# A recurrent mixer's triangular solve in packed halves on ScalarE, GpSimd and TensorE, and a second weight buffer for early queries

## The chip, the cores and the metric

One NeuronCore of a Trainium2 chip runs the whole program. The engines are TensorE (PE; its weight loads are listed as PEld), VectorE (DVE), ScalarE (ACT), GpSimd (POOL) and SyncE (SP), each with a queue that it works off in order, and 16 DMA engines. The metric is the device time of one launch in microseconds (us). [...]

## What is computed

One layer of a decoder for 1024 prompt tokens and 64 sample tokens, as tiles 0 to 7 of 128 tokens and tile 8 of 64:

```
proj = rmsnorm(h) @ w_in                      # retention part and RWKV part
o_ret = retention(q, k, v)                    # chunks of 128 tokens, state between chunks
for t: sa = S @ (-kk[t])                      # RWKV-7, 8 heads of 64
       S = S * exp(log_w[t]) + outer(sa, kk[t]*a[t]) + outer(v[t], k[t]);  y[t] = S @ r[t]
h = h + concat(o_ret, o_rw) @ w_out
q = rmsnorm(h) @ peer_wq; s = q . keys        # 8 heads x 2 x 128 keys
e, gsm = top 16 of the sums of the two top 16 lists          # 128 experts for each token
h = h + sum_e gelu(x . u_tab[e]) * gsm_e * v_tab[e]
h = h + sigmoid(rmsnorm(h) @ ple_gate) * (p @ ple_proj);  y = rmsnorm(h)
```

The RWKV recurrence of a 128-token chunk is a triangular system for each head: with the strictly triangular matrix Q of the chunk, U solves (1 - Q) U = X, and the state and y follow from U.

## The kernel before

**Stages.** The program is written as generators that are stepped in turn, and a scheduler then sets each engine's order from the dependencies, the order of writing and its own model of durations. From 0 to about 545 us the projections of tiles run (`group_a`), with the mixer of tile 0. Then `group_b` runs the mixers of tiles 1, 8, 2, 3, 4, 5, 6, 7: at each step one yield of the solve and end of one tile (`cur`), one of the beginning of the next tile (`nxt`), one of the output projection of a finished tile (`c_rows`), and one of `early`. About 1868 us the queries of tiles 2 to 7 begin (`c_query`). Then the first 96 of 128 blocks of the dense experts are computed (`hidden`: 24 matmuls each), beside the top-k of tiles 2 to 7 and the gates of tiles 4 to 7 (`gates`: one-hot rows `oh` by VectorE, scaled by ScalarE, multiplied by TensorE into `pwt`). About 2819 us `dense_fused` and then `dense_stored` begin; the end (`ple`) starts about 3771 us.

**The gathers.** Tiles 0, 1, 8 (in `early`) and 2, 3 (later) take their experts by indirect DMA: GpSimd issues `grow` (512 KB, 128 rows) at L1126, VectorE multiplies it with x and sums (L1140, table u) or adds it to an accumulator (L1154, table v). For 0, 1, 2, 3 that is 128 of each table, for tile 8 it is 64 of each: 1152 gathers. The early ones have four `grow` buffers (five for tile 8, whose query is done). In the queues of GpSimd and VectorE they stand among the instructions of `group_b`.

**The early queries** (`early_query`) make the scores of tiles 0, 1 and 8. For each of 16 key sets a weight `ewq` of 512 KB is loaded, 8 matmuls `epq` are made with it, then one with the keys. Those of tiles 1 and 8 run in `group_b`, with one buffer `Wq` for the weights: the next load waits for the last matmul on the one before.

**The solve.** In `rw_mix` after `yield "chain"`, Z (128 x 8 heads x 128) starts as 1 plus Q's diagonal blocks of 2 (L824 on VectorE, L825 on GpSimd). Five levels m = 2, 4, 8, 16, 32 double the block, each in two groups of four heads (s = 0, 1): TensorE transposes Z (`trz`, L837), ScalarE copies it to `Tt` (L839), TensorE multiplies N (the transpose of Q) with the second half of each block (`pG`, L842), VectorE masks the product into `G` (L844), TensorE multiplies (`pZG`, L849), and VectorE adds the result into Z (L851). After five levels Z holds the inverses of two blocks of 64; U is then made in two halves (L901, L895, L897 on VectorE, L901, L903). Tiles 0 to 7 have five levels, tile 8 two.

Of the kernel before, what the change touches and what calls it, by code (L numbers as in the profile page):

```python
# [44 lines left out]
def consts():  # L45
# [27 lines left out]
    for i, m in enumerate(LEVELS):  # L73
        for qq in range(64):
            b = qq // m
            lev[b * 2 * m:b * 2 * m + m, i, qq] = 1.0
# [134 lines left out]
class K:  # L211
# [46 lines left out]
    def setup_mix(self, es):  # L258
# [18 lines left out]
        self.Sb = [[cp.tile([128, 4, 128], F32, name=f"S{a}{b}") for b in range(2)] for a in range(3)]  # L277
        for a in self.Sb:
            for b in a:
                nc.gpsimd.memset(b, 0.0)  # L280
        self.Sret = self.Swkv = None
# [364 lines left out]
    def group_b(self, tiles, early):  # L646
# [3 lines left out]
        with ExitStack() as e:  # L650
# [6 lines left out]
                                  ("PC", [64, 8, 8], F32, 1), ("Z", h8, F32, 2), ("N", h8, F32, 2), ("Tt0", [128, 4, 128], F32, 1),  # L657
                                  ("Tt1", [128, 4, 128], F32, 1), ("G0", [128, 4, 64], F32, 1), ("G1", [128, 4, 64], F32, 1)])
# [35 lines left out]
    def rw_mix(self, t):  # L694
# [123 lines left out]
        N = wp.tile([128, 8, n], F32, name="N", bufs=b2)  # L818
        self.transposes_n(N, Q[:, :, 0], n)
        yield  # L820
        Z = wp.tile([128, 8, n], F32, name="Z", bufs=b2)
        bd = self.c("bdiag2", n)[:, None, :n].to_broadcast([n, 8, n])
        idb = self.c("ident", n)[:, None, :n].to_broadcast([n, 8, n])
        nc.vector.tensor_tensor(Z[:n, :, :n], Q[:n, :, 0, :n], bd, op=OP.mult)  # L824
        nc.gpsimd.tensor_tensor(Z[:n, :, :n], Z[:n, :, :n], idb, op=OP.add)  # L825
        yield "chain"
        lev = self.c("lev").rearrange("p (l q) -> p l q", l=5)
        nq = n // 2
        for li, m in enumerate(LEVELS):
            if smp and m >= 8:  # L830
                break
            Zs = Z[:n, :, :n].rearrange("p h (c s m) -> p h c s m", s=2, m=m)[:, :, :, 1, :]
            Tt, G, pz = [None] * 2, [None] * 2, [None] * 2
            for s in range(2):
                p = self.ps("trz", hb[s]).rearrange("p (a b) -> p a b", a=4)
                for j in range(4):
                    nc.tensor.transpose(p[:n, j, :n], Z[:n, 4 * s + j, :n], self.c("ident", n)[:, :n])  # L837
                Tt[s] = wp.tile([128, 4, n], F32, name=f"Tt{s}")
                nc.scalar.activation(Tt[s][:n, :, :n], p[:n, :, :n], AF.Copy)  # L839
                p = self.ps("pG", hb[s])[:, :256].rearrange("p (h q) -> p h q", h=4)  # L840
                for j in range(4):
                    nc.tensor.matmul(p[:n, j, :nq], N[:n, 4 * s + j, :n], Zs[:, 4 * s + j], start=True, stop=True)  # L842
                G[s] = wp.tile([128, 4, n // 2], F32, name=f"G{s}")
                nc.vector.tensor_tensor(G[s][:n, :, :nq], p[:n, :, :nq], lev[:n, li, None, :nq].to_broadcast([n, 4, nq]), op=OP.mult)  # L844
                yield
            for s in range(2):
                p = self.ps("pZG", hb[s])[:, :256].rearrange("p (h q) -> p h q", h=4)
                for j in range(4):
                    nc.tensor.matmul(p[:n, j, :nq], Tt[s][:n, j, :n], G[s][:n, j, :nq], start=True, stop=True)  # L849
                pz = p[:n, :, :nq].rearrange("p h (c m) -> p h c m", m=m)  # L850
                nc.vector.tensor_tensor(Zs[:, 4 * s:4 * s + 4], Zs[:, 4 * s:4 * s + 4], pz, op=OP.add)  # L851
                yield
# [357 lines left out]
    def early(self, wp):  # L1210
# [4 lines left out]
        for t in E0[1:]:  # L1215
# [327 lines left out]
```

## Time and profile before

| | us |
|---|---|
| median of 3 runs | 3937.49 (3921.43 to 3937.65) |
| the profiled execution | 3941.76 |
| its span | 3940.0 |
| PE busy | 3367.7 (85%) |
| DVE busy | 2961.7 (75%) |
| POOL busy | 2339.6 (59%) |
| ACT busy | 1225.5 (31%) |

The span is the time from the first to the last instruction of the profiled execution. A busy time is the sum of an engine's instructions; "PEclk" is the TensorE clock that was granted, as a share of full speed, and the DMA share is the mean busy share of the 16 DMA engines. A wait is put down to what released it last. A stage is read from its own busy shares and waits, and the share of an engine over the whole span says little about one stage.

### The profile page before, as it was taken

The page shows a single profiled execution, that of the slowest core. Times are in us where ns is not written, and L with a number is a line of the kernel's source. Part 1 is how long each engine was busy: PE and PEld are TensorE (multiplying, and loading weights), DVE is VectorE, ACT ScalarE, POOL GpSimd, SP SyncE. Part 2 cuts the span into 40 slices and gives each one's busy share as a digit, 9 for nine tenths or more (in the row PEclk, how much of TensorE's full clock was granted, in tenths as well). Part 3 has the DMA queues.
Part 4 walks back from the last instruction along what each step waited for, and adds up shares of the span by engine and source line. Part 5 has one row for each costly group of instructions (what it writes and reads, how often), then busy time and mean ns, then how long its engine had stood idle before and what let it go on. Part 6 is the DMA issues. An engine that isn't in the chain of part 4 may idle for free.

```text
span 3940.0 us, 52682 instructions
## 1 busy us (share of the span) xinstructions
PE 3367.7 (85%) x17749; PEld 2768.7 (70%) x17749; DVE 2961.7 (75%) x5764; ACT 1225.5 (31%) x2247; POOL 2339.6 (59%) x2051
## 2 busy tenths in 40 slices
PE   8798985777869776885899899999699988999978
PEld 7687984645747664763788678888588866677757
DVE  4454488977697689886659999987777777777774
ACT  4232221011111111111232266777422333333322
POOL 5353175544454536554567757886488777777740
PEclk9799995666977567676999999999899999999989
DMA  7267568898868878789998748899899999999962
GB/s 256 72 194 234 168 209 266 277 302 267 295 229 285 299 269 283 265 278 332 331 350 295 245 171 302 306 347 344 324 343 341 334 362 357 358 362 349 339 230 70
DMA packets 473864, 1107.20 MB, mean 281 GB/s; under 512 B 74555, under 2 KB 191545, under 8 KB 467642
## 3 DMA queue, kind: packets, MB, share of 16 engines
q0 software_dynamic: 165888, 604.05, 43.0%
q1 hardware_dynamic: 245694, 393.26, 30.5%
q10 hardware_dynamic: 62012, 106.52, 7.2%
q8 instruction: 141, 2.31, 0.2%
q14 instruction: 129, 1.06, 0.1%
HBM read 997.17 MB, written 106.43 MB: 280 GB/s over the span
## 4 chain that ended last, share of the span: by engine, by line
PE 45%; DVE 22%; DMA 16%; issue 7%; POOL 6%; ACT 2%; SPq 0%; ACTq 0%; POOLq 0%; DVEq 0%
PE py L1294 14%; DVE grow L1140 4%; DVE gacc L1154 3%; PE ph L325 3%; PE ph L326 3%; PE ph L327 3%; POOL grow L1126 3%; DMA ewq<-in_wq 2%; PE epq L1194 2%; DMA grow<-in_pv,eid 2%; DMA grow<-in_pu,eid 2%; POOL vl L300 2%; DMA ft<-fd 1%; DVE oh L1240 1%; PE ewo L610 1%
## 5 line engine op out<-in xcount | busy, mean ns | idle before, releaser
L1126 POOL DMA_INDIRECT grow<-in_pv,eid x576 | 569.8, 989 | 507.3 <-DVE gacc L1154 309.4
L1126 POOL DMA_INDIRECT grow<-in_pu,eid x576 | 568.7, 987 | 435.2 <-DVE grow L1140 287.9
L1154 DVE SCALAR_TENSOR_TENSOR gacc<-grow,ac,gacc 128x1024 f32<-128x1024 f32 x571 | 731.8, 1282 | 89.5 <-DMA grow<-in_pv,eid 84.3
L1140 DVE SCALAR_TENSOR_TENSOR grow<-grow,gacc 128x1024 f32<-128x1024 f32 x576 | 691.1, 1213 | 125.0 <-DMA grow<-in_pu,eid 118.3
L1294 PE MATMUL py<-ah,vh 128*128 128x512 f32 x1024 | 408.1, 399 | 40.3 <-ACT ah L296 27.1
L1294 PE MATMUL py<-ah,vl 128*128 128x512 f32 x1024 | 407.1, 403 | 34.1 <-POOL vl L300 34.0
L325 PE MATMUL ph<-cx,uh 128*128 128x512 f32 x1024 | 406.4, 397 | 7.2 <-ACT geh L1262 7.2
L326 PE MATMUL ph<-cx,uh 128*128 128x512 f32 x1024 | 406.4, 397 | 0.0
L327 PE MATMUL ph<-cx,ul 128*128 128x512 f32 x1024 | 405.5, 396 | 1.0 <-POOL ul L300 1.0
L1294 PE MATMUL py<-al,vh 128*128 128x512 f32 x1024 | 405.3, 396 | 0.0
L300 POOL TENSOR_TENSOR vl<-vraw,vh 128x640 fp32r<-128x640 f32 (+2 forms) x224 | 325.4, 1457 | 53.1 <-ACT vh L296 49.3
L300 POOL TENSOR_TENSOR ul<-uraw,uh 128x1024 fp32r<-128x1024 f32 x128 | 308.6, 2412 | 64.5 <-ACT uh L296 62.3
L296 ACT ACTIVATE vh<-vraw 128x640 fp32r<-128x640 f32 (+2 forms) x224 | 154.9, 692 | 393.8 <-PE py L1294 238.3
L1294 PEld LDWEIGHTS py<-ah,vl 128*128 128x128 f32 x1024 | 194.1, 190 | 98.4 <-POOL vl L300 56.1
L1294 PEld LDWEIGHTS py<-ah,vh 128*128 128x128 f32 x1024 | 194.6, 190 | 96.5 <-ACT vh L296 28.7
L1298 DVE TENSOR_TENSOR yT<-yT,py 128x512 f32<-128x512 f32 x216 | 147.4, 684 | 151.5 <-PE py L1294 151.1
L325 PEld LDWEIGHTS ph<-cx,uh 128*128 128x128 f32 x1024 | 194.7, 190 | 48.4 <-ACT geh L1262 8.8
L1294 PEld LDWEIGHTS py<-al,vh 128*128 128x128 f32 x1024 | 194.0, 189 | 43.7
L327 PEld LDWEIGHTS ph<-cx,ul 128*128 128x128 f32 x1024 | 194.9, 190 | 41.6 <-POOL ul L300 1.9
L326 PEld LDWEIGHTS ph<-cx,uh 128*128 128x128 f32 x1024 | 195.0, 190 | 39.1
L296 ACT ACTIVATE uh<-uraw 128x1024 fp32r<-128x1024 f32 x128 | 135.2, 1056 | 246.1 <-PE ph L326 128.5
L300 POOL TENSOR_TENSOR wl<-wraw,wh 128x1024 fp32r<-128x1024 f32 x45 | 110.5, 2455 | 138.8 <-ACT wh L296 138.7
(400 smaller groups left out, 7833.3 us busy)
## 6 DMA issues: line engine op xcount, KB each, us to landing
uraw<-in_puT SPq DMA_DIRECT2D x128, 512.0 KB, 4.8
vraw<-in_pvd SPq DMA_DIRECT2D x152, 320.0 KB, 6.1
cw<-in_w_out SPq DMA_DIRECT2D x128, 256.0 KB, 5.1
wd<-wst ACTq DMA_DIRECT2D x32, 1024.0 KB, 13.1
wt<-wd SPq DMA_DIRECT2D x64, 512.0 KB, 8.0
wraw<-in_w_ret SPq DMA_DIRECT2D x48, 512.0 KB, 4.7
ewq<-in_wq SPq DMA_DIRECT2D x48, 512.0 KB, 6.7
gd<-geh ACTq DMA_DIRECT2D x96, 256.0 KB, 5.0
```

The lines of the kernel that those rows point to most:

```text
L296: nc.scalar.activation(hi, src, AF.Copy)
L300: nc.gpsimd.tensor_tensor(lo, src, hi.bitcast(F32), op=OP.subtract)
L325: mm(out, lh(k), rh(k), start=first and k == 0, stop=False)
L326: mm(out, lh(k), rl(k), start=False, stop=False)
L327: mm(out, ll(k), rh(k), start=False, stop=last and k == nk - 1)
L610: nc.tensor.matmul(p[:n], oT[k // 4][:, k % 4, :n], w, start=k == 0, stop=k == 7)
L1126: nc.gpsimd.indirect_dma_start(out=g, out_offset=None, in_=src, in_offset=bass.IndirectOffsetOnAxis(ap=self.eid[t][:, j:j + 1], axis=0))
L1140: nc.vector.scalar_tensor_tensor(g[:, c], g[:, c], 1.0, x[:, c], op0=OP.mult, op1=OP.mult, accum_out=hv[:, i, j:j + 1])
L1154: nc.vector.scalar_tensor_tensor(y[:, c], g[:, c], ac[:, j:j + 1], y[:, c], op0=OP.mult, op1=OP.add)
L1194: nc.tensor.matmul(p[:, :n], w[:, k], xT[:, k, :n], start=k == 0, stop=k == 7)
L1294: nc.tensor.matmul(p, lh[:, b, :], rh, start=b == 0 and j == 0, stop=b == nb - 1 and j == 2)
L1298: nc.vector.tensor_tensor(yT[:, d, :], yT[:, d, :], p, op=OP.add)
```

## The change

1. **The solve.** Z is kept in two packed halves (`Zt[0][:, 0]` the first halves of all blocks, `[:, 1]` the second ones) in one of two buffers Z0, Z1 that swap at each level. The mask moves from the product to N: GpSimd makes `Nm` (128 x 256) ahead (`mask`). ScalarE copies `pG` to `G` in two instructions of 64 partitions, into the diagonal quarters of a tile that was set to zero once. The transposes take two heads at once (two instead of four), TensorE adds the old half by a product with the identity (256 columns) in front of the two products of `Tt` and `G`, so that ScalarE only copies the sum out (`new`), and GpSimd copies the unchanged half to the other buffer (`old`), each in two instructions for m below 64. A sixth level m = 64 joins the two blocks of 64, with no mask and no copy by GpSimd. U then comes from one round (`pU`, 16 matmuls, one copy). VectorE has no part in the levels. The state product S0 is made ahead of the levels.
2. **Buffers.** `Wq` in the pool of the early queries has two buffers, and the queries of tiles 1 and 8 use both. `Tt`, `G`, Z, N and one of the states have fewer or smaller ones.

The rest is unchanged. The core of the diff (line numbers of the kernel after are 2 to 53 higher):

```diff
@@ rw_mix
-        lev = self.c("lev").rearrange("p (l q) -> p l q", l=5)
-        nq = n // 2
-        for li, m in enumerate(LEVELS):
...
-            for s in range(2):
-                p = self.ps("trz", hb[s]).rearrange("p (a b) -> p a b", a=4)
-                for j in range(4):
-                    nc.tensor.transpose(p[:n, j, :n], Z[:n, 4 * s + j, :n], self.c("ident", n)[:, :n])
...
-                nc.vector.tensor_tensor(G[s][:n, :, :nq], p[:n, :, :nq], lev[:n, li, None, :nq].to_broadcast([n, 4, nq]), op=OP.mult)
-                yield
...
-                nc.vector.tensor_tensor(Zs[:, 4 * s:4 * s + 4], Zs[:, 4 * s:4 * s + 4], pz, op=OP.add)
-                yield
+        def mask(i):
+            if i < len(steps) and levels[steps[i][0]] < 64:
...
+                Nm[i] = wp.tile([128, 4, nq], F32, name="Nm", bufs=1 + b2)
+                nc.gpsimd.tensor_tensor(Nm[i][:n].rearrange("p h (c m) -> p h c m", m=m),
...
+        old = lambda d, a: nc.gpsimd.tensor_copy(d, a)
+        new = lambda d, a: nc.scalar.activation(d, a, AF.Copy)
...
+        for i, (li, s) in enumerate(steps):
...
+            for j in range(4):
...
+                if m == 64:
+                    nc.tensor.matmul(po_, N[64:, h, 0:64], Zl[64:, 1, h], start=True, stop=True)
+                else:
+                    nc.tensor.matmul(po_, Nm[i][:n, j], Zl[:, 1, h], start=True, stop=True)
...
+                for e in (0, 64):
+                    es_ = slice(e, e + 64)
+                    nc.scalar.activation(G[es_, :, es_], p[es_, :256].rearrange("p (a b) -> p a b", a=2)[:, :, es_], AF.Copy)
+            if m < 64:
+                moved(old, Zl[:, 0, 4 * s:4 * s + 4], m, 0, s)
+            mask(i + 2)
...
+            for j in range(0, 4, w):
+                f = Zl[:, 0, 4 * s + j:4 * s + j + w].rearrange("p h q -> p (h q)")
+                nc.tensor.transpose(p[:nq * w, j // w, :n], f, idn)
+            nc.scalar.activation(Tt[s][:nq * w, :, :n], p[:nq * w, :4 // w, :n], AF.Copy)
+            yield
...
+            for s in range(2):
...
+                nc.tensor.matmul(p[:n, :, :nq], idn, zs, start=True, stop=False)
...
+                for j in range(0, 4, w):
+                    nc.tensor.matmul(p[:n, j:j + w, :nq], Tt[s][:nq * w, j // w, :n], G4[:nq * w, j:j + w, :nq], start=False, stop=j + w == 4)
+                if m < 64:
+                    moved(new, p[:n, :, :nq], m, 1, s)
+                else:
+                    new(zs, p[:n, :, :nq])
+                yield
@@ early, build
-            for _ in self.early_query(wp, t, "Wq", 1, ("Wq", "xT")):
+            for _ in self.early_query(wp, t, "Wq", 2, ("Wq", "xT")):
...
-            self.layout(ep0, [("V", [128, D], F32, 2), ("W", [128, D], F32, 1), ("xy", [128, D], F32, 1), ("Wq", [128, D], F32, 1), ("xT", [128, D], F32, 1)])
+            self.layout(ep0, [("V", [128, D], F32, 2), ("W", [128, D], F32, 1), ("xy", [128, D], F32, 1), ("Wq", [128, D], F32, 2), ("xT", [128, D], F32, 1)])
```

What stands in the queues at three places, before and after (a row is a line of the kernel, an operation, out<-in, its shape and how many follow one another):

VectorE, the first levels of tile 4's solve, before; `grow` rows are sums of the gather of tile 1:

```order
L1140 SCALAR_TENSOR_TENSOR grow,hv<-grow,gacc 128x1024 x13
L844 TENSOR_TENSOR G_10375<-pG,cstb 128x256
L844 TENSOR_TENSOR G_10409<-pG,cstb 128x256
L1140 SCALAR_TENSOR_TENSOR grow,hv<-grow,gacc 128x1024 x4
L851 TENSOR_TENSOR Z<-Z,pZG 128x128x2
L1140 SCALAR_TENSOR_TENSOR grow,hv<-grow,gacc 128x1024
L851 TENSOR_TENSOR Z<-Z,pZG 128x128x2
```

VectorE at the same place, after:

```order
L800 TENSOR_TENSOR Kq<-pab,cstb 128x512
L1207 SCALAR_TENSOR_TENSOR gacc<-grow,ac,gacc 128x1024 x3
L814 TENSOR_TENSOR nbk<-ptk,rn_10060 128x512
L1193 SCALAR_TENSOR_TENSOR grow,hv<-grow,gacc 128x1024 x16
L1034 TENSOR_TENSOR hnx<-hnx,pgt 128x512
```

The solve's rows are gone from the queue, and the gather beside this tile is 28 sums further back, still at the end of tile 0's list (`gacc`) before tile 1's begins.

GpSimd, tile 4 from the start of Z to the end of the levels, before:

```order
L974 TENSOR_TENSOR hnx<-hnx,bv 128x512
L825 TENSOR_TENSOR Z<-Z,csta 128x1024
L1126 DMA grow<-in_pu,eid_65 128x1024 x67
L290 TENSOR_SCALAR hnr<-hnss 128x8
L291 TENSOR_TENSOR hnr<-hnr,halves 128x8
```

GpSimd in the levels m = 2 to 8 of the same tile, after:

```order
L1179 DMA grow<-in_pu,eid_65 128x1024 x4
L869 COPY Z_10743<-Z_10626 128x32x4 x2
L1179 DMA grow<-in_pu,eid_65 128x1024 x2
L848 TENSOR_TENSOR Nm<-N,cstb 128x256
L869 COPY Z_10743<-Z_10626 128x32x4 x2
L848 TENSOR_TENSOR Nm<-N,cstb 128x256
L1179 DMA grow<-in_pu,eid_65 128x1024 x2
L869 COPY Z_10904<-Z_10743 128x16x8 x2
```

One run of 67 gathers becomes runs of one to eight with the solve's masks and copies between them.

TensorE in the third of the four tiles' gates, before (`ph` are matmuls of `hidden`):

```order
L327 MATMUL ph<-cx_13025,ul 128x512
L1245 MATMUL pwt<-oh_20393,oh_20394 128x128 x4
L1245 MATMUL pwt<-oh_20412,oh_20413 128x128 x4
L325 MATMUL ph<-cx_13025,uh 128x512
L326 MATMUL ph<-cx_13026,uh 128x512
```

TensorE at the same gates, after:

```order
L1298 MATMUL pwt<-oh_20733,oh_20734 128x128 x4
L1298 MATMUL pwt<-oh_20752,oh_20753 128x128 x4
L1298 MATMUL pwt<-oh_20771,oh_20772 128x128 x4
L1298 MATMUL pwt<-oh_20790,oh_20791 128x128 x4
L1298 MATMUL pwt<-oh_20809,oh_20810 128x128 x4
```

Of the 128 groups of gates, the last 80 now stand behind the last `ph` of the first 96 blocks; before, no more than the last 16 did.

## Rows read from the trace of the kernel before

**Rows 1.** Windows, one per stage: engines' busy us and instructions, granted clock, DMA share, GB/s

```profile
core 0: us, PE busy (x) PEld busy (x) DVE busy (x) ACT busy (x) POOL busy (x), PEclk, DMA share, GB/s
0.00:545.00 545.00, 475.25 (x3646) 451.73 (x3647) 264.97 (x604) 165.91 (x282) 235.25 (x220) 0.93 0.56 180
545.00:1868.00 1323.00, 992.23 (x5281) 775.99 (x5280) 1055.06 (x1965) 186.31 (x405) 685.88 (x678) 0.69 0.83 281
1868.00:2269.00 401.00, 366.46 (x1852) 307.15 (x1850) 324.54 (x982) 117.41 (x170) 266.49 (x207) 0.97 0.86 305
2269.00:2819.00 550.00, 490.87 (x2562) 415.85 (x2562) 481.26 (x1115) 385.79 (x786) 374.37 (x274) 0.96 0.81 296
2819.00:3771.00 952.00, 903.55 (x3776) 709.08 (x3776) 733.11 (x965) 325.39 (x523) 747.23 (x625) 0.99 0.98 348
```

**Rows 2.** DVE groups, 545 to 1868 us: shapes, count | busy us, mean ns | idle before

```profile
L1154 DVE SCALAR_TENSOR_TENSOR gacc<-grow,ac,gacc 128x1024 f32<-128x1024 f32 x245 | 313.9, 1281 | 57.7 <-DMA grow<-in_pv,eid 55.9
L1140 DVE SCALAR_TENSOR_TENSOR grow<-grow,gacc 128x1024 f32<-128x1024 f32 x256 | 308.0, 1212 | 69.3 <-DMA grow<-in_pu,eid 67.8
L844 DVE TENSOR_TENSOR G<-pG,cstb 128x256 f32<-128x256 f32 x70 | 29.2, 417 | 29.4 <-PE pG L842 29.1
L851 DVE TENSOR_TENSOR Z<-Z,pZG 128x256 f32<-128x256 f32 x70 | 28.6, 413 | 11.2 <-PE pZG L849 10.6
```

**Rows 3.** Line L897, the add between the halves of U: ns min/median/max

```profile
L897 DVE TENSOR_TENSOR X<-X,pL x8: 691/691/692, 218.9 to 1789.0; 64x512 f32<-64x512 f32 x8
```

**Rows 4.** Chain of waits, 545 to 1868 us by line, then pieces in the second query

```profile
by line: issue 8.7%; DVE grow L1140 7.2%; DMA ewq<-in_wq 6.6%; DMA grow<-in_pu,eid 5.5%; DMA grow<-in_pv,eid 5.4%; PE epq L1194 5.1%; DVE gacc L1154 4.7%; DMA ft<-fd 4.0%; POOL grow L1126 4.0%; PE ewo L610 2.9%; DMA cw<-in_w_out 2.7%; PE pZ
...
1371.97 3.69 PE epq L1194 x16
1375.68 7.57 DMA ewq<-in_wq
1383.29 3.69 PE epq L1194 x16
1387.00 7.73 DMA ewq<-in_wq
1394.77 3.68 PE epq L1194 x16
```

**Rows 5.** Window of tiles 3 and 4 in the mixer stage, columns as in rows 1

```profile
1144.00:1498.00 354.00, 276.43 (x1320) 226.71 (x1320) 272.76 (x636) 48.40 (x112) 178.94 (x177) 0.63 0.81 276
```

**Rows 6.** PE groups, 545 to 1868 us, of the solve and of a 256-column product

```profile
L842 PE MATMUL pG<-Z,N 128*128 128x64 f32 x560 | 89.3, 314 | 0.0
L837 PE MATMUL trz<-csta,Z 128*128 128x128 f32 x280 | 55.3, 331 | 5.9 <-POOL Z L825 3.0 <-DVE Z L851 2.7
L793 PE MATMUL pab<-art,k 64*128 64x256 f32 x112 | 52.4, 648 | 14.6 <-DVE Q L803 6.9 <-DVE Kq L798 6.6 <-ACT es L1198 1.1
```

**Rows 7.** POOL and ACT groups of the whole span near the new ones

```profile
L549 POOL TENSOR_TENSOR fdst<-rb 128x256 f32<-128x256 f32 x28 | 26.2, 938 | 19.3 <-ACT rb L544 17.0 <-DMA fd<-fdst 2.2
L393 POOL TENSOR_TENSOR retd<-ropeA,ropeB 128x128 f32<-128x128 f32 x32 | 17.7, 554 | 0.0
L1196 ACT ACTIVATE eqT<-epq 128x128 f32<-128x128 f32 x32 | 8.9, 277 | 102.4 <-PE epq L1194 87.7 <-DMA out_wkv_s<-sw 7.2 <-PE pZG L849 6.7
```

**Rows 8.** Waits of POOL in 560 to 1880 us: total, times, longest

```profile
POOL grow L1126 <- DVE gacc L1154: 249.7, 156, 13.3
POOL grow L1126 <- DVE grow L1140: 207.1, 156, 11.1
```

**Rows 9.** Windows of L1154's instructions: DVE busy (count), clock, DMA share, GB/s

```profile
545.00:1868.00 1323.00, 313.86 (x245) 0.69 0.83 281
1868.00:2269.00 401.00, 91.88 (x72) 0.97 0.86 305
2269.00:2819.00 550.00, 10.31 (x8) 0.96 0.81 296
```

**Rows 10.** Windows after the mixer stage, columns as in rows 1

```profile
2100.00:2600.00 500.00, 465.18 (x2262) 386.10 (x2262) 486.15 (x1531) 280.98 (x516) 368.65 (x264) 0.98 0.76 268
```

More of the change, by code (lines that the diff above doesn't have):

```diff
@@ L73, in consts @@
     for i, m in enumerate(LEVELS):
-        for qq in range(64):
-            b = qq // m
-            lev[b * 2 * m:b * 2 * m + m, i, qq] = 1.0
+        a = q // m * 2 * m + q % m
+        lev[:, i] = (p[:, None] // (2 * m) == a[None] // (2 * m)) & (p[:, None] // m % 2 == 1)
     put("lev", lev)
@@ L276, in setup_mix @@
         self.lnb = self.row(cp, 'ln_b')
-        self.Sb = [[cp.tile([128, 4, 128], F32, name=f"S{a}{b}") for b in range(2)] for a in range(3)]
+        self.Sb = [[cp.tile([128, 4, 128], F32, name=f"S{a}{b}") for b in range(1 + (a < 2))] for a in range(3)]
         for a in self.Sb:
@@ L280, in setup_mix @@
                 nc.gpsimd.memset(b, 0.0)
+        self.G = [cp.tile([128, 2, 128], F32, name=f"G{s}") for s in range(2)]
+        for g in self.G:
+            nc.gpsimd.memset(g, 0.0)
         self.Sret = self.Swkv = None
@@ L817, in rw_mix @@
             yield
-        N = wp.tile([128, 8, n], F32, name="N", bufs=b2)
+        N = wp.tile([128, 8, n], F32, name="N")
         self.transposes_n(N, Q[:, :, 0], n)
         yield
[L821 to L825, printed above, removed]
@@ new lines, in rw_mix @@
+        Zt = [wp.tile([128, 8 * n], F32, name="Z0"), None]
+        pairs = lambda a: a.rearrange("p h (c s m) -> p h c s m", s=2, m=2)
+        shp = [n, 8, n // 4, 2]
+        bd, idb = (pairs(self.c(k, n)[:, None, :n]) for k in ("bdiag2", "ident"))
+        for s in range(2):
+            zd = Zt[0][:n].rearrange("p (s h c m) -> p s h c m", s=2, h=8, m=2)[:, s]
+            nc.vector.tensor_tensor(zd, pairs(Q[:n, :, 0, :n])[:, :, :, s], bd[:, :, :, s].to_broadcast(shp), op=OP.mult)
+            nc.gpsimd.tensor_tensor(zd, zd, idb[:, :, :, s].to_broadcast(shp), op=OP.add)
@@ L857, in rw_mix @@
                 nc.vector.tensor_tensor(S0[ps_, :, ps_], self.Swkv[ps_, :, ps_], pe[ps_, 0, :, None].to_broadcast([64, 4, 64]), op=OP.mult)
+        lev = self.c("lev").rearrange("p (l q) -> p l q", l=5)
+        nq = n // 2
+        levels = [m for m in LEVELS + (64,) if not smp or m < 8]
+        steps = [(li, s) for li in range(len(levels)) for s in range(2)]
+        Nm = {}
+        def mask(i):
+            if i < len(steps) and levels[steps[i][0]] < 64:
+                li, s = steps[i]
+                m = levels[li]
+                Nm[i] = wp.tile([128, 4, nq], F32, name="Nm", bufs=1 + b2)
+                nc.gpsimd.tensor_tensor(Nm[i][:n].rearrange("p h (c m) -> p h c m", m=m),
+                                        N[:n, 4 * s:4 * s + 4, :n].rearrange("p h (c s m) -> p h c s m", s=2, m=m)[:, :, :, 0],
+                                        lev[:n, li, None, :nq].rearrange("p h (c m) -> p h c m", m=m).to_broadcast([n, 4, nq // m, m]), op=OP.mult)
@@ new lines, in rw_mix, with moved @@
+        mask(0)
+        mask(1)
+        idn = self.c("ident", n)[:, :n]
+        def moved(eng, src, m, s, g):
+            src = src.rearrange("p h (c m) -> p h c m", m=m)
+            h0 = 4 * g
+            if m * 2 < n and not (smp and m == 4):
+                dst = Zt[1][:n].rearrange("p (b h c s m) -> p b h c s m", b=2, h=8, s=2, m=m)
+                src = src.rearrange("p h (c b) m -> p b h c m", b=2)
+                for b in range(2):
+                    eng(dst[:, b, h0:h0 + 4, :, s], src[:, b])
+            else:
+                dst = Zt[1][:n].rearrange("p (h c s m) -> p h c s m", h=8, s=2, m=m)
+                eng(dst[:, h0:h0 + 4, :, s], src)
@@ L859, in state_mm @@
+        if smp:
+            for s in range(2):
+                nc.gpsimd.memset(self.G[s], 0.0)
         def state_mm(p, hp, j):
```

90 lines of the change are left out of this document (44 added, 46 removed).

## The prediction

> **What bounds the kernel now.** I read the stages first [rows 1]. From 2819 us on TensorE is 95% busy at a clock of 0.99 and the DMA engines are at 0.98: nothing in the change touches that stage, except for the gathers that are left over for it. From 0 to 545 us TensorE is 87% busy, and only the small solve of tile 0 is touched. The change works between 545 and 1868 us (stage B, 1323 us). There VectorE is busiest with 1055 us (80%), the DMA engines stand at 0.83, TensorE at 75% with a clock of 0.69 of full speed, GpSimd at 52%, ScalarE at 14%. No engine is full; all work off their queues in order and wait for each other. Of VectorE's 1055 us, 622 are gather sums and only some 63 the solve [rows 2, 3]. So the solve's own time on VectorE is small; what it couples is large, because a gather sum in front of it in the queue delays the solve, and a solve step that waits for TensorE delays the gathers (29 us of idle in front of L844).
>
> The chain of waits [rows 4] names a second cause: in B 6.6% of it, 87 us, is the load of `ewq`. In the query of tile 8 a load of 7.6 us and eight matmuls of 3.7 us alternate, since one buffer holds the weights; 16 such rounds make 180 us. That is where the gather gets far ahead of the mixer: 67 gathers stand in one run in GpSimd's queue.
>
> After B, from 1868 to 2819 us (stages C and D, 951 us), TensorE is 90% busy, and VectorE is at 97% from 2100 to 2600 us [rows 10]. A delay of VectorE there is a delay of the gates, and `dense_fused` needs them.
>
> **Part 1, VectorE's own work in B.** Seven full solves lie in B: 70 x 0.417 + 70 x 0.413 + 7 x 0.691 = 63 us go [rows 2, 3]. The start of Z is made in two halves now, about nothing more.
>
> **Part 2, the gathers move.** I counted in VectorE's queue how many gather sums stand ahead of three points: the first weight of `c_query` (the end of B), the first gate, and the first dense activation. Before: 503, 640, 777. After: 424, 640, 794. The profile agrees with the count of before: 256 sums of table u and 245 of v in B, and two that begin a sum of v [rows 2, 9]. So 79 sums of v leave B, at 1.281 us each: 101 us. They are not saved: C has 216 sums instead of 137, D 154 instead of 137, together 96 more, 123 us. Behind the first dense activation the count is lower by 17.
>
> VectorE in B: 1055 - 63 - 101 = 891 us. Its idle time in B is 268 us. The wait for `ewq` shrinks with the second buffer, but new waits come (below), so I keep the 268: B would take 1159 us, **163 us less**. Check with TensorE: per half level four transposes, four pG and four pZG of about 0.32 us (3.8 us) become two transposes, four pG, one product of 256 columns (0.648) and two products of 128 (0.331 each), 3.2 us [rows 6]; 70 of these save 43 us, the sixth level (14 halves of 3.0) costs 42, and one round for U instead of two about -10. So TensorE keeps its 992 us, less some 10: 982 / 1159 = 85% busy. It was at 78% over tiles 3 and 4 [rows 5]; 85% is more than any long stretch of B shows, so this is near the limit at this clock, and I don't go beyond 163.
>
> **Part 3, what takes the solve over.** ScalarE: per half level two copies into G, two or one into Z, less half of Tt, about 1 us at 0.277 us a copy [rows 7], 70 us in all on an engine with 186 busy of 1323. Hidden. GpSimd: per half level a mask (0.938, the 128x256 row) and two copies of 128 columns (between nothing and the 0.554 of the two-input row; I take 0.5), 1.9 us, 136 us for seven tiles; 79 gather issues of 1.0 us leave. 686 + 57 = 743 of 1159 us, 64%. As busy time it is hidden. As a queue it is not sure: GpSimd stood 457 us in B waiting for VectorE to free a `grow` buffer, 312 times, up to 13 us [rows 8], and a mask or copy behind such a gather waits as long. I price this below as a rival; in the forecast it is part of the idle time that I kept.
>
> **Part 4, C and D.** VectorE was busy 325 + 481 = 806 us and idle 145 us [rows 1]; it gets 123 us more, 929. If the idle time stays at 145 the two stages take 1074 us (+123). If VectorE ran at the 97% of rows 10 throughout, 958 us (+7). The truth is nearer the first: in the first part of C the gathers come at the transfers' pace and little else stands in the queue, and in D the last 80 of 128 gate groups now have no `hidden` matmuls beside them, so that each waits for VectorE, ScalarE and TensorE in turn. I take an idle time of 110: 1040 us, **89 us more**.
>
> **Part 5, the rest.** In the stage from 2819 to 3771 us the queue holds 355 sums instead of 352: nothing. Twenty sums no longer stand behind the last addition to yT; tile 3's rows are the last that the end needs, and before they came in time, so nothing either. The first stage: the solve of tile 0 leaves VectorE, which is at 49% there; nothing, within 10 us.
>
> **Sum.** -163 + 89 = -74 us against the profiled execution's 3941.76: 3868. The median shown is 4 below that execution, inside the spread of the runs, and I leave the sum at 3868.
>
> **The rivals.**
> *TensorE holds B.* If TensorE cannot be pushed beyond the 78% of rows 5, B takes 982 / 0.78 = 1259 us, 64 less, and with +89 the time is 3967, 25 more than before; anything between 78 and 85% lies between this and the forecast. For it: the clock of 0.63 in that stretch and the chains between in-order queues. Against it: that stretch held the `ewq` rounds, which go.
>
> *GpSimd's queue becomes the chain (slower).* Each half level now needs GpSimd's copies before the next level's transposes, and its masks before pG. If each of 70 half levels waits once for the mean of rows 8 (457 / 312 = 1.5 us), and that is no longer hidden by the other tile's work, 105 us come back: 163 - 105 = 58 less in B, 89 more in C and D, 3973. It decides from about 70 us of such waits on. For it: the queue after shows masks and copies between single gathers. Against it: the masks are made two halves ahead, and what VectorE did before stood behind sums of the same length.
>
> *VectorE takes the extra sums in C and D almost free.* With +15 instead of +89: 3794. For it: the first 136 us of C, where it was only partly busy. Against it: the 97% of rows 10.
>
> *The clock rises in B.* [...] If filled gaps bring B to C's clock, TensorE's work shrinks to 982 x 0.69 / 0.97 = 699 us, VectorE alone holds B, and at the 87% share that it reaches in D [rows 1] B takes 891 / 0.87 = 1024 us, 299 less: 3732. [...] I give it little, since B's TensorE still waits for three other engines at every level.
>
> That the change doesn't do what it says is no case: the queues show the solve gone from VectorE.
>
> **How the numbers follow.** Forecast 3868, 0.50, its own range 3835 to 3910; TensorE holds B, 3967, 0.16; GpSimd's queue, 3973, 0.14; free sums in C and D, 3794, 0.12; clock, 3732, 0.08. A measurement tells about 0.5% from no change, 20 us: faster is below 3918, slower above 3957. Faster: 0.50 + 0.12 + 0.08 less 0.04 of the forecast's upper edge = 0.66. Same: that 0.04 and over half of the first rival, which shades into the forecast, 0.13. Slower: the rest of it and GpSimd's case, 0.21. The range goes from 3790 to 3975: it holds the forecast, the first rival, the free sums and about half of GpSimd's case, and leaves out the clock and the other half.
>
> **What would show each step.** B's end (first split of a `c_query` weight) at about 1705 instead of 1868 us; VectorE busy about 890 us in it, with 424 gather sums; pieces of `ewq` loads almost gone from the chain. First dense activation at about 2745 instead of 2819 us, with VectorE above 90% and TensorE waiting for gates just ahead of it. GpSimd's queue: if the solve waits in it, TensorE's transposes and pG show idle time released by GpSimd's copy and mask, above 70 us in sum, and B ends after 1790 us. The clock: B's granted clock above 0.85. The prediction is wrong if B gains less than C and D lose, or if the last stage no longer takes 952 us.

## The result and the profile after

| | before | after |
|---|---|---|
| median | 3937.57 us (3921.43 to 3940.35) | 3979.32 us (3973.33 to 3998.84) |
| ratio to before, 95% interval | | 1.0122 (1.0084 to 1.0159) |
| the profiled execution, its span | 3941.76, 3940.0 | 3998.84, 3997.1 |

The change made the kernel slower; 3868 was forecast, in a range up to 3975. The profiled execution of after is the longest of its four; its stages are compared with [rows 1], and what a change is worth in time is read from the ratios. The windows of after, with the columns of [rows 1]: stage A, B (to the first split of a `c_query` weight), C (to the first gate), D (to the first dense activation) and E.

```profile
0.00:547.00 547.00, 476.93 (x3634) 450.77 (x3635) 243.56 (x584) 176.35 (x329) 242.62 (x251) 0.92 0.56 179
547.00:1782.00 1235.00, 921.09 (x5107) 679.17 (x5106) 909.47 (x1738) 251.10 (x743) 699.23 (x831) 0.72 0.81 268
1782.00:2422.00 640.00, 581.78 (x2733) 476.70 (x2732) 551.29 (x1523) 176.70 (x246) 467.26 (x351) 0.96 0.88 301
2422.00:2878.00 456.00, 334.48 (x1685) 289.58 (x1683) 404.32 (x670) 322.67 (x710) 265.49 (x222) 0.81 0.86 310
2878.00:3833.00 955.00, 902.99 (x3775) 709.35 (x3775) 736.47 (x966) 324.92 (x524) 746.40 (x624) 0.99 0.98 347
```

B is 88 us shorter (1235 against 1323), C and D together 145 us longer (1096 against 951), A and E within 3 us. Neither engine that bound before got more to do ahead of the dense part: VectorE is busy 2109 us there against 2126, TensorE 2314 against 2325. The loss is idle time, and VectorE's lies ahead of C: it idles 58 us more in B and 23 more in A (where it has 21 us less to do in the same time), but 5 us less in C and D, which are longer because 150 us more of its work stands in them. In D TensorE stands 122 of 456 us, and its granted clock is 0.81 where it was 0.96.

Where the waiting begins is seen in VectorE's timeline (start, length, engine, line, operation, out<-in, idle before). `ac<-ac,gsm` follows the 128 sums of table u of tile 0, of tile 1, then the 64 of tile 8; the `gacc<-grow` row ends with the 640th gather sum; `it` is the first gate. Before:

```profile
833.25 0.28 DVE L1146 TENSOR_TENSOR ac<-ac,gsm 128x128 f32<-128x128 f32 x1
1550.85 1.74 DVE L1146 TENSOR_TENSOR ac<-ac,gsm 128x128 f32<-128x128 f32 x1 [0.67 <-ACT ac L1145]
2031.58 0.23 DVE L1146 TENSOR_TENSOR ac<-ac,gsm 128x64 f32<-128x64 f32 x1 [2.97 <-ACT ac L1145]
2259.56 1.27 DVE L1154 SCALAR_TENSOR_TENSOR gacc<-grow,ac,gacc 128x1024 f32<-128x1024 f32 x1
2268.81 0.26 DVE L1233 COPY it<-pit 128x128 f32<-128x128 f32 x1
```

After:

```profile
873.17 0.28 DVE L1199 TENSOR_TENSOR ac<-ac,gsm 128x128 f32<-128x128 f32 x1
1666.52 0.29 DVE L1199 TENSOR_TENSOR ac<-ac,gsm 128x128 f32<-128x128 f32 x1 [0.62 <-ACT ac L1198]
2211.76 2.03 DVE L1199 TENSOR_TENSOR ac<-ac,gsm 128x64 f32<-128x64 f32 x1 [0.32 <-ACT ac L1198]
2416.52 3.93 DVE L1207 SCALAR_TENSOR_TENSOR gacc<-grow,ac,gacc 128x1024 f32<-128x1024 f32 x3
2422.28 0.28 DVE L1286 COPY it<-pit 128x128 f32<-128x128 f32 x1
```

While the mixers got ahead, the gathers fell behind: 40 us after the first 128, 116 after the second table u, 180 at tile 8, 153 at the first gate. The gates use the memory of the early gathers and wait for all 640 sums of these; the 640th ends at 2261 us before and at 2420 after, 8 and 2 us ahead of the gate. By then 72 of the first 96 `hidden` blocks are done, 35 before, so the last gates run alone. TensorE's `pwt` in the last stretch of D (2700 to 2819 us before, to 2878 after; busy, mean ns, idle before them) shows it, first before, then after:

```profile
L1245 PE MATMUL pwt<-oh,oh 128*128 128x128 f32 x256 | 42.6, 318 | 13.8 <-ACT oh L1242 13.8
```

```profile
L1298 PE MATMUL pwt<-oh,oh 128*128 128x128 f32 x340 | 71.4, 381 | 45.4 <-ACT oh L1295 42.4 <-DVE oh L1293 2.9
```

One reason why the gathers are slower stands in GpSimd's queue in B (count, busy, mean ns, idle before and what ended it). After:

```profile
L1179 POOL DMA_INDIRECT grow<-in_pu,eid x253 | 251.5, 994 | 234.5 <-DVE grow L1193 157.5 <-issue 23.3 <-ACT gacc L1187 14.1
L1179 POOL DMA_INDIRECT grow<-in_pv,eid x172 | 177.4, 1032 | 194.9 <-DVE gacc L1207 133.3 <-issue 11.3 <-DVE es L1097 11.1
L848 POOL TENSOR_TENSOR Nm<-N,cstb 128x256 f32<-128x256 f32 (+1 forms) x74 | 48.8, 671 | 46.2 <-ACT N L694 23.8 <-PE pG L887 21.8
L869 POOL COPY Z<-Z 128x128 f32<-128x128 f32 (+2 forms) x146 | 40.4, 308 | 21.8 <-ACT Z L870 14.0 <-PE pZG L910 7.0
```

The masks and copies are 89 us of work, and GpSimd stands another 68 us in front of them until ScalarE or TensorE are that far. All this time the next gather is queued behind, though its buffer may be free. The waits for VectorE to free a buffer fell (134 and 162 against 250 and 207 in [rows 8]): GpSimd now comes late more often. A buffer's round is short enough to feel it. The median from issue to landing is 5.8 us (547 to 830 us, before), an issue keeps GpSimd busy for 1.0 (0.99 to 1.03 in the rows above) and a sum takes 1.2; with four buffers and 2.25 us per gather a round is 9.0 us. Pairing each sum with the issue that reuses its buffer, the gap between them is 0.62, 0.63 and 0.57 us on average in the first three lots of 128 gathers before, and 0.90, 1.24 and 1.46 after; a gather takes 2.25, 2.96 and 2.45 us before, 2.54, 3.17 and 2.91 after. That is only part of the delay: a round, from one issue into a buffer to the next, grew from 9.0, 11.8 and 10.1 us to 10.2, 12.9 and 12.1, and of these 1.2, 1.1 and 2.0 us the gap is 0.3, 0.6 and 0.9. Most of the rest lies between landing and sum (1.4, 3.3 and 1.8 us before, 1.9, 3.9 and 3.2 after, where the trace tells the landing). VectorE comes to the sums later: in B VectorE's waits for gathers fell from 124 to 115 us, those for ScalarE rose from 33 to 69 and for TensorE from 93 to 112. How far this too follows from GpSimd's queue is not shown.

### The profile page after: what moved, and what is told of

It is laid out like the page before. It is cut to its first block, busy times and chain, and to the rows that moved or that the text cites. A ratio compares the mean times of both kernels' runs of the same rounds, so it can differ in the third digit from the quotient of the medians.

```text
span 3997.1 us, 53069 instructions
## 1 busy us (share of the span) xinstructions
PE 3358.8 (84%) x17565; PEld 2716.6 (68%) x17565; DVE 2925.9 (73%) x5597; ACT 1296.2 (32%) x2631; POOL 2434.4 (61%) x2313
## 4 chain that ended last, share of the span: by engine, by line
PE 37%; DVE 17%; DMA 12%; issue 7%; POOL 6%; ACT 3%; ACTq 0%; SPq 0%; POOLq 0%; DVEq 0%
PE py L1347 13%; DVE grow L1193 4%; POOL grow L1179 3%; PE ewo L612 2%; DMA grow<-in_pu,eid 2%; POOL vl L302 2%; DVE gacc L1207 2%; PE pwt L1298 2%; PE ph L327 2%; PE ph L329 2%; PE ph L328 2%; DMA grow<-in_pv,eid 2%; DMA cw<-in_w_out 1%; DVE eq L1134 1%; PE pq L327 1%
## 5 line engine op out<-in xcount | busy, mean ns | idle before, releaser
L1193 DVE SCALAR_TENSOR_TENSOR grow<-grow,gacc 128x1024 f32<-128x1024 f32 x576 | 689.5, 1211 | 110.5 <-DMA grow<-in_pu,eid 97.9
L1298 PE MATMUL pwt<-oh,oh 128*128 128x128 f32 x1024 | 187.3, 346 | 96.2 <-ACT oh L1295 93.1
L1298 PEld LDWEIGHTS pwt<-oh,oh 128*128 128x128 f32 x1024 | 170.6, 243 | 117.2 <-ACT oh L1295 115.1
L327 PEld LDWEIGHTS ph<-cx,uh 128*128 128x128 f32 x1024 | 195.9, 191 | 52.2 <-ACT uh L298 7.4
```

Of the source, the lines that this page charges most:

```text
L327: mm(out, lh(k), rh(k), start=first and k == 0, stop=False)
L1193: nc.vector.scalar_tensor_tensor(g[:, c], g[:, c], 1.0, x[:, c], op0=OP.mult, op1=OP.mult, accum_out=hv[:, i, j:j + 1])
L1298: nc.tensor.matmul(pw[:, j, :], oh[1][:, j, :], oh[0][:, j, :], start=True, stop=True)
```

## The experiments

Each row was timed beside runs of the kernel before. B's end, the end of the 640th sum and the first gate are from the profiled execution, in us (first `wql`, the sums in VectorE's order, first `it`). The expectations name an earlier time for the 640th sum, 2226 us before and 2386 after: these are the ends of the 633rd and the 628th. The diffs show the core of each edit, without the lines on buffer counts and layout.

| kernel | median | ratio to before | B's end | 640th sum | first gate |
|---|---|---|---|---|---|
| before | 3938 | | 1868 | 2261 | 2269 |
| after | 3979 | 1.0122 (1.0084 to 1.0159) | 1782 | 2420 | 2422 |
| e1 solve alone | 4006 | 1.0160 (1.0122 to 1.0199) | 1848 | 2382 | 2384 |
| e2 buffer alone | 3987 | 1.0132 (1.0084 to 1.0180) | 1775 | 2358 | 2369 |
| e3 masks, copies off GpSimd | 3952 | 1.0043 (1.0021 to 1.0066) | 1750 | 2367 | 2372 |
| e4 solve, 5 row buffers | 3928 | 0.9988 (0.9967 to 1.0009) | 1861 | 2226 | 2234 |
| e5 before, single N | 3949 | 1.0048 (1.0020 to 1.0076) | 1838 | 2268 | 2273 |
| e6 before, GpSimd loaded | 3990 | 1.0143 (1.0105 to 1.0180) | 1890 | 2318 | 2319 |
| e7 after, 40 gathers fewer | 3908 | 0.9943 (0.9918 to 0.9969) | 1762 | 2276 (600th) | 2284 |
| e8 as e4, off GpSimd | 3933 | 0.9999 (0.9977 to 1.0021) | 1843 | 2249 | 2254 |
| e9 before, 5 row buffers | 3960 | 1.0079 (1.0054 to 1.0104) | 1891 | 2127 | 2229 |
| e10 solve, 6 row buffers | 3922 | 0.9969 (0.9948 to 0.9990) | 1885 | 2109 | 2213 |
| e11 both parts, 5 row buffers | 3937 | 1.0016 (0.9993 to 1.0040) | 1811 | 2262 | 2274 |
| e12 before, VectorE loaded | 3985 | 1.0135 (1.0105 to 1.0165) | 1897 | 2307 | 2321 |
| e13 after, VectorE loaded | 3986 | 1.0136 (1.0095 to 1.0177) | 1771 | 2409 | 2411 |
| e14 after, masks off | 3961 | 1.0075 (1.0046 to 1.0104) | 1746 | 2395 | 2398 |
| e15 after, copies off | 3964 | 1.0100 (1.0062 to 1.0137) | 1752 | 2391 | 2395 |
| e16 before, GpSimd waits | 3957 | 1.0075 (1.0042 to 1.0108) | 1853 | 2298 | 2304 |
| e17 e10, copies off | 3948 | 1.0036 (1.0016 to 1.0057) | 1888 | 2152 | 2241 |
| e18 e11, copies off | 3925 | 0.9983 (0.9969 to 0.9997) | 1827 | 2249 | 2258 |

**One part alone.** e1 is the changed kernel with one `Wq` buffer; e2 the kernel before with two; e5 is e2's control, since N had to give up a buffer for the room.

```diff
# e1, from after
-            for _ in self.early_query(wp, t, "Wq", 2, ("Wq", "xT")):
+            for _ in self.early_query(wp, t, "Wq", 1, ("Wq", "xT")):
# e5, from before (e2: this and two buffers for Wq)
-... ("Z", h8, F32, 2), ("N", h8, F32, 2), ...
+... ("Z", h8, F32, 2), ("N", h8, F32, 1), ...
```

> The new solve, with one buffer for the early query weights as before; 462 gather sums stand ahead of the first c_query weight (503 before, 424 after). Three theories. Gather chain: the first gates wait for 640 gather sums, these come through a ring of four row buffers, and GpSimd, which issues them in order, now has the solve's masks and copies (some 110 us of work and 68 us of waits) between them; then the 640th sum ends near 2386 us as in the changed kernel (2226 before) and the time is 3955 to 3990 us. Deferred sums: the loss in the stages after the mixers goes by the sums that leave the mixers' stage, 41 here against 79; about half of the 145 us, against a gain without the 78 us of the second buffer: 3990 to 4030 us. Output rows: the loads of the output projection hold the end of the mixers' stage; then this kernel keeps the first kernel's 370 us there and loses only the buffer's 78 us: about 4050 us.

> The old solve on VectorE, with the two buffers for the early query weights; to make room the tile N of the solve has one buffer instead of two. 445 gather sums stand ahead of the first c_query weight. Gather chain: GpSimd carries no work of the solve, so the 640th sum stays within 30 us of 2226 us and the time is 3900 to 3945 us. Deferred sums: 58 of them leave the mixers' stage, some 105 us of loss against 78 us of gain in the stretch of the early query: about 3965 us. Output rows: as the changed kernel in its last stretch, 3935 to 3960 us.

> The kernel before with one buffer instead of two for the tile N of the solve, nothing else; all three kernels of the first series whose 640th gather sum came near 2330 us have this single buffer. If the single N is what slows them: the 640th sum near 2320 us and a time of 3970 to 3990 us. If it is not (and the second buffer of the early query itself is what slowed the kernel with the buffer alone): the 640th sum within 30 us of 2226 us, 3920 to 3950 us.

The solve alone is slower than the change as a whole by its median, and B shrinks by 20 us only. The 640th sum came 38 us earlier than in the changed kernel, where the gather theory had it at the same time, and the time was above its 3990; 4006 lies in the range of the deferred sums. The buffer alone shortens B as it was meant to (1838 to 1775, against e5), but moves the 640th sum from 2268 to 2358, and ends slower than e5, with intervals apart, and above all three ranges expected. On the new solve it takes off 27 us by the medians, with intervals that overlap. The single N costs a little, 0.2 to 0.8%, without moving the 640th sum much.

**GpSimd.** e3 takes the solve's masks and copies off it, e14 the masks alone, e15 the copies alone; e6 puts as much work on it in the kernel before, e16 a wait almost without work.

```diff
# e3 (e14: the first, e15: the second), from after
-                nc.gpsimd.tensor_tensor(Nm[i][:n]...
+                nc.vector.tensor_tensor(Nm[i][:n]...
-        old = lambda d, a: nc.gpsimd.tensor_copy(d, a)
+        old = lambda d, a: nc.scalar.activation(d, a, AF.Copy)
# e6, from before, at each half level
+                nc.gpsimd.tensor_tensor(Dm[:n, :, :nq], N[:n, 4 * s:4 * s + 4, :nq], lev[...], op=OP.mult)
+                for _ in range(2):
+                    nc.gpsimd.tensor_copy(Dm[:n, :2, :nq], N[:n, 4 * s:4 * s + 2, :nq])
# e16, from before, at each half level
+                nc.gpsimd.tensor_copy(Dm[:n, :, :8], Tt[s][:n, :, :8])
```

> The changed kernel with the solve's masks on VectorE and its copies of the kept half on ScalarE, so that GpSimd has none of the solve but the first addition; 432 sums ahead of the first c_query weight (424 in the changed kernel). Gather chain with GpSimd's queue as its brake: the gathers keep the pace of before, the 640th sum ends by about 2280 us, and the time falls below 3925 us. Deferred sums: VectorE gets 20 to 30 us more and nothing is gained: 3975 to 4010 us. Output rows: no change, 3960 to 3990 us.

> The kernel before, its solve on VectorE untouched, with GpSimd given idle work at each half level as the changed kernel gives it: one product of 128x256 and two copies of 128x128 of the tile N into a scratch tile that nobody reads. Gather chain with GpSimd's queue as its brake: the first 128 gathers take 2.45 to 2.55 us each instead of 2.25, the 640th sum comes 50 to 110 us later than 2226, the time is 3960 to 3990 us. If GpSimd's added work is hidden: within 12 us of 3935 us.

> The changed kernel with the masks alone moved from GpSimd to VectorE (84 of 0.64 us, which waited 54 us for ScalarE's N and TensorE's pG in GpSimd's queue); the copies stay. If the waiting in the queue is what costs: most of the 27 us that came off with both, 3950 to 3965 us. If it goes by work alone: half of it, less VectorE's new 30 us, about 3975 to 3990 us.

> The changed kernel with the kept half's copies alone moved from GpSimd to ScalarE (160 of 0.29 us, which waited 28 us for ScalarE and TensorE); the masks stay. By work: 46 us less on GpSimd at 0.5 us of the end per us (56 for some 105 in the kernel before), 3950 to 3960 us. By waiting: a third of the waits, 3965 to 3975 us.

> The kernel before with one small GpSimd copy (128x32) at each half level of what ScalarE has just written of the transposes (Tt), into a scratch tile that nobody reads: 84 copies, under 20 us of work in all, but each stands in GpSimd's queue until the solve gets there. If waiting in the queue in front of the gathers' issues is a brake: 20 to 50 us slower than before, the 640th sum after 2270 us. If only work counts: within 12 us of 3934.

GpSimd's idle work in B of e6 (groups as above), then e16's copies over the whole span (duration ns min/median/max) and what GpSimd waited for in front of them:

```profile
L847 POOL COPY Dm<-N 128x128 f32<-128x128 f32 (+1 forms) x148 | 48.8, 330 | 3.6
L845 POOL TENSOR_TENSOR Dm<-N,cstb 128x256 f32<-128x256 f32 (+1 forms) x74 | 47.2, 638 | 13.2 <-ACT N L692 10.4
```

```profile
L845 POOL COPY Dm<-Tt x84: 199/210/1099, 164.6 to 1768.9; 128x32 f32<-128x32 f32 x80, 64x32 f32<-64x32 f32 x4
its engine sat idle before it (us, times) until:
  ACT Tt L839: 64.0, 40
```

Ninety-six us of work that nobody needs cost 1.43% (56 us), and the 640th sum is 57 us late. The delay is not where it was expected: the first 128 gathers take 2.31 us each, not 2.45 to 2.55, and it comes later (the third lot takes 2.68 us against 2.45). In e16, 64 us of waiting with some 18 us of work go with a 640th sum that is 37 us late and 0.75% more time. That the waiting costs it is not shown: VectorE idled no more ahead of the dense part than in the kernel before (688 us against 693), and the same instructions kept it busy longer (2151 against 2126).

Taking the changed kernel's masks and copies off (to VectorE and ScalarE) brings 0.8% back, with intervals apart from after's. Stage B of e3:

```profile
547.00:1750.00 1203.00, 903.65 (x5109) 667.85 (x5108) 943.90 (x1820) 283.25 (x889) 621.37 (x619) 0.73 0.84 279
```

VectorE's idle time in B is 259 us, against 326 in the changed kernel and 268 in the one before. A gather takes 2.28 us again in the first 128, but 3.14 and 2.77 in the next two lots. The two halves alone point the same way, each with an interval that overlaps after's. GpSimd's masks and copies thus cost time; whether by work or by waiting is open, and e3 stayed above the 3925 that was expected, so they are not all of it.

**VectorE.** The same idle work on VectorE, in the kernel before (e12) and in the changed one (e13).

```diff
# e12, from before, at each half level (e13, from after: four of 128x112)
+                for _ in range(2):
+                    nc.vector.tensor_tensor(Dm[:n, :, :nq], N[:n, 4 * s:4 * s + 4, :nq], lev[...], op=OP.mult)
```

> The kernel before with idle work on VectorE: two products of 128x256 at each half level of the solve, into a scratch tile that nobody reads, 168 in all, some 60 us on the engine that the change relieved of 63. The prediction's first step (VectorE's busy time sets the length of the mixers' stage): that stage gets 50 to 60 us longer, the time is 3975 to 4000 us. Gather chain: VectorE's time in that stage is not the bound, the stage grows by less than 25 us, the 640th sum moves by less than 30 us, 3925 to 3955 us.

> The changed kernel with idle work on VectorE: four products of 128x112 at each half level but the last, into a scratch tile that nobody reads, 50 to 80 us in all. If VectorE's time counts as in the kernel before (0.76 us of the end per us of work, 53 for 70): 40 to 60 us slower than the changed kernel, 4015 to 4040 us. If the relief was worth nothing because VectorE had stopped to be the limit: within 15 us of 3979.

The idle work's group in B and then stage B's window, of e12 and below it of e13:

```profile
L846 DVE TENSOR_TENSOR Dm<-N,cstb 128x256 f32<-128x256 f32 (+1 forms) x148 | 66.2, 448 | 6.3 <-ACT N L692 3.2 <-ACT X L882 2.6
```

```profile
545.00:1897.00 1352.00, 1009.46 (x5240) 790.69 (x5240) 1100.07 (x2103) 184.33 (x401) 681.75 (x671) 0.67 0.83 273
```

```profile
L899 DVE TENSOR_TENSOR Dm<-N,cstb 128x112 f32<-128x112 f32 (+1 forms) x296 | 105.4, 356 | 32.2 <-ACT N L694 27.8
```

```profile
547.00:1771.00 1224.00, 914.96 (x5050) 672.91 (x5050) 994.76 (x2031) 250.31 (x739) 708.21 (x828) 0.72 0.82 270
```

In the kernel before, 66 us more on VectorE make B 29 us longer, each of the later points late, and the end 1.35% (53 us) later: VectorE's time did count, so the relief was worth something, by the same rate some 48 us for the 63 (an estimate). In the changed kernel 105 us more change nothing: B takes 1224 instead of 1235 us, and the ratio is 1.0136 against 1.0122. VectorE is no longer the limit of B there.

**The ring of gather buffers.** e4 uses the second `Wq`'s 4 KB as a fifth row buffer; e10 has six, e11 five and both weight buffers (both with one buffer for the masks); e9 gives the kernel before five. e7 leaves out gathers, e8 and e17, e18 move GpSimd's part as above.

```diff
# e4, from e1 (e9, from e5; e10: one more)
-        rows = ("V", "V", "W", "xy")
+        rows = ("V", "V", "W", "xy", "Vx")
# e7, from after, table v
-        for j in range(n):
+        for j in range(n - 40 * (t == 8)):
```

> The new solve with one buffer for the early query weights, and the freed 4 KB as a fifth row buffer for the gathers (four before); 507 sums ahead of the first c_query weight. Gather chain: the ring sets the pace, so a fifth buffer brings the 640th sum to 2200 us or earlier, and the time to 3840 to 3910 us. Deferred sums: with 507 sums in the mixers' stage the later stages are as before (951 us), the mixers' stage is as in the solve alone: 3900 to 3950 us. If neither the ring nor the sums bind: as the solve alone, within 15 us.

> The changed kernel without the last 40 v gathers and sums of tile 8 (that tile's output lacks these terms). Gather chain: the first gate waits for the last of the early sums, so it comes 40 x 3.35 us earlier, at about 2290 instead of 2422 us; by the other kernels the first dense activation follows 0.4 of a shift of the gates, so the time is 3915 to 3940 us. VectorE as the bound of those stages: the gates come 40 x 1.28 = 51 us earlier, at 2370 us, and the time falls by about the same 51, less what fills it: 3925 to 3950 us. If neither: 3970 us.

> New solve, one buffer for the early query weights, a fifth row buffer for the gathers, and the solve's masks on VectorE and its kept copies on ScalarE. Gather chain: the two gains add, 3928 less the 27 us that came off when GpSimd was relieved, 3885 to 3915 us, the 640th sum by 2150 us, faster than the kernel before. If the ring was the only brake: as with the fifth buffer alone, 3920 to 3945 us.

> The kernel before, its solve on VectorE, with one buffer for the tile N and the room used for a fifth row buffer of the gathers (the single N alone measured 3949 us). Gather chain: the ring is what sets the pace in the kernel before too, the 640th sum comes by 2170 us (2247 with the single N alone), and the time is 3860 to 3915 us. If the ring binds only where GpSimd carries the solve: 3935 to 3955 us.

> The new solve, one buffer for the early query weights, six row buffers for the gathers; to make room the masks Nm have one buffer instead of three. Gather chain: a sixth buffer brings less than the fifth (which took 78 us off), the 640th sum by 2130 us (2158 with five), 3890 to 3925 us. If five were enough: 3925 to 3950 us.

> The changed kernel, both its parts, with a fifth row buffer for the gathers; the masks Nm have one buffer instead of three. Gather chain: the shorter mixers' stage now meets a faster ring, the 640th sum comes near 2250 us (2386 with four), and the time is 3890 to 3930 us. Output rows as the bound of the mixers' stage: that stage ends at 1780 us again and the time stays above 3940 us.

> The new solve with six row buffers (3922 us) and the kept half's copies moved from GpSimd to ScalarE (15 us off in the changed kernel). If the brakes add: 3900 to 3912 us, clearly faster than the kernel before. If a longer ring already covers GpSimd's queue: 3915 to 3930 us.

> Both parts of the change with five row buffers (3937 us) and the kept half's copies on ScalarE. If the brakes add: 3915 to 3927 us. If the longer ring covers GpSimd's queue: 3930 to 3945 us.

The first gate of e7:

```profile
2284.02 0.27 DVE L1286 COPY it<-pit 128x128 f32<-128x128 f32 x1
```

Forty gathers fewer bring the first gate 138 us forward (134 was expected of the gather chain, 51 of VectorE's time): the first gate did wait for the last early sum. The end comes 1.8% earlier (3908 us, below the 3915 to 3940 expected). In e4 a fifth buffer takes 1.7% off e1, and e10 is faster than the kernel before by 0.3%, the fastest of these that compute everything. Then the case turns. In e9 the 640th sum comes 140 us earlier than in e5 and the first gate 45 us, and nothing is won. Stages B and C of e9, and of e10:

```profile
544.00:1891.00 1347.00, 1010.55 (x5259) 797.04 (x5258) 1088.76 (x2018) 187.41 (x404) 712.04 (x708) 0.67 0.84 288
1891.00:2229.00 338.00, 312.53 (x1625) 264.98 (x1624) 262.67 (x816) 100.30 (x150) 205.32 (x164) 0.96 0.81 289
```

```profile
544.00:1885.00 1341.00, 933.48 (x5078) 682.23 (x5077) 1052.40 (x1877) 255.04 (x743) 803.70 (x942) 0.71 0.84 291
1885.00:2213.00 328.00, 304.67 (x1590) 258.72 (x1589) 258.42 (x815) 99.67 (x148) 199.15 (x158) 0.96 0.80 289
```

With early gathers the first gate no longer follows the 640th sum, as it does by 1 to 14 us in the other kernels: in e9, e10 and e17 it comes 89 to 104 us after the sum, and 328 to 353 us after B's end. But the first gate alone does not set the end, as e9 shows. What the 20 traces show instead is what a gather sum costs that B leaves over. From the first dense activation to the end all take 1110 to 1135 us. In C and D together VectorE idles 127 to 163 us in all of them, so their length goes by the work that is left for it: it is 575 us plus 1.41 us for each sum in them, within 18 us (274 sums and 951 us before, 370 and 1096 after). A sum itself takes 1.2 to 1.3 us.

So the question is what a sum costs in B. In the kernel before, VectorE is the limit there: e9 does 36 more sums in B than e5 (534, 498), B gets 53 us longer, and C and D 50 us shorter. With the new solve e4 does 45 more than e1 (507, 462), B gets 13 us longer, and C and D 110 us shorter. The change freed VectorE in B, but the gathers did not come fast enough to use it, and 79 sums were left over from B; where the ring is deeper (e4, e10, e11), the freed time is used, and the loss is gone. This is the "deferred sums" of the expectations, though its ranges fit e1 and e4 and missed e2 and e3; the gather chain's ranges of the time, given for e1 to e4 and e6 to e12, were met by e6 (at the edge) and e10 alone.

e17 and e18 did not settle whether ring and queue add: the copies off GpSimd cost 0.7% with six buffers and took 0.3% off with five and two weight buffers; e8 gained nothing. Every edit also lets the scheduler set a new order on all queues, and effects of that size, also the 0.75% of e16 and the 0.48% of e5, may be its doing. That was not separated.

## Why the prediction was wrong

- **Part 1 (63 us leave VectorE): right in size, and it had a value in the kernel before** (by e12, an estimate of 48 us).
- **Part 2, the move of the sums: right. "I keep the 268" of idle time: wrong.** VectorE was busy 909 us in B, forecast 891; its idle time grew to 326, and B shrank by 88 instead of 163. The step took VectorE's busy time plus a constant as the stage's length. e13 shows that after the change busy time no longer sets it. Of the 133 us by which the dense part starts later than forecast (2878, not 2745), 76 are lost here, 58 of them idle time.
- **TensorE's share as a bound: not reached.** 921 of 1235 us is 75%, the same share as before: what I held for possible (85%) was not reached. The first rival, TensorE at 78%, comes closest in B's length (1259); but TensorE's share there is a result, as B reaches 1203 us in e3 with the same 75%.
- **Part 3, "as busy time it is hidden": the step that failed.** GpSimd was busy 699 us in B, 57%, less than the 743 that I allowed, and yet not hidden: with its masks and copies elsewhere VectorE's idle time in B is 259 us instead of 326 and the loss 0.4% instead of 1.2% (e3), and work of that size on GpSimd costs the kernel before 1.4% (e6). I looked for who in the solve would wait for GpSimd, and not for who stands behind the solve in GpSimd's queue. The rows were there: in [rows 8] GpSimd waits for the buffer of each gather to come free, so it issues as soon as that is so, and a late issue takes from the ring's slack, which is small (a landed gather waits 1.4 to 3.3 us for its sum there).
- **GpSimd's rival: the right engine, the wrong victim, a near number by chance.** TensorE's waits for the masks and copies in B sum to 12 us, not 70; the issues of the gathers came late instead, which is part of their delay.
- **Part 4: 89 forecast, 145 measured, the other 56 us.** VectorE was busy 956 us in C and D (929 forecast) and idle 140 (110 forecast, 145 before). The 96 sums were right; the 35 us that I took off the idle time were not there, and in none of the 20 kernels did it fall to 110. The cover that I saw go, the `hidden` blocks beside the last gates, is gone as described (in the traces 86 of the 128 groups of gates come behind the first 96 blocks, 26 before, where the queues gave me 80 and 16); and the gates started late, behind the gathers' chain, which I did not follow to its end.
- **The second buffer.** The `ewq` loads did leave the chain of waits, and that shortened B (e2); its price, a later 640th sum, I did not see. Why the gathers are slower beside the denser queries (2.28, 3.26 and 2.74 us each in e2, 2.20, 2.85 and 2.46 in e5), with no new work on GpSimd, stays open.
- **Free sums, the clock: no.** B's clock is 0.72. No run shows that filled gaps bring B to C's clock, the term in the 3732: in the windows of B given here the clock lies between 0.67 (e9, e12) and 0.73 (e3), with TensorE 70 to 75% busy in all of them. **Part 5: right**; stage E takes 955 us, against 952.

Put together for the solve alone, with prices measured in the other kernel: about -48 for VectorE's relief, +56 for GpSimd's work, +19 for the single N, 27 us against the 63 of e1's ratio. The 30 us of e16 would fill most of the rest, but their cause is open. The prices are not independent, so this proves no sum.

## What to carry to other kernels

Before work is moved to an engine with idle time, ask what else that engine issues: a queue that feeds a short ring of DMA buffers can be on the path at a modest busy share, here 57%. When a stage gets shorter, count what it leaves to the next one and what that costs there: here 1.41 us for each gather sum, about the sum's own time. Idle work put on one engine at a time, in both kernels, prices the engines better than their busy shares, as long as the price is well above what a new order on the queues alone can do.

## What the runs showed of the hardware

- An indirect gather of 512 KB lands 5.8 us after its issue before and 5.6 after (medians of table u, 547 to 830 us), 6.8 and 6.0 of table v (830 to 1250 us), with the DMA engines at 0.79 to 0.84 in these windows. At one gather per 2.25 us (the first 128, before) two to three are in flight at a time, an estimate from 5.8 over 2.25; no run shows one alone.
- GpSimd's copy of 128x128 takes 0.31 us and its two-input product of 128x256 0.67 us in B, against the 0.5 and 0.938 that I took from [rows 7]: the work was smaller than forecast and cost more.
- VectorE's `eq` product (72 times, most over 128x800) took 1181 ns in the mean before and 1461 ns after: 20 us more for the same work. The traces show what goes with it. Where GpSimd did no arithmetic beside a full-size `eq`, it took 962 to 1042 ns (40 of 64 before, 31 after); beside GpSimd's arithmetic it took up to 3129 ns before and 3793 after, which makes 14 us in sum before and 34 after. The gather sums, whose second tensor lies in PSUM, took the same with and without it (table u before: 1211 ns and 1214).
